# Two layers of a hybrid trunk on one core: the q/k products issued in halves of 256 tokens

## The chip, the cores and the metric
The kernel runs on one core of one Trainium2 chip. Its engines are TensorE (products; the profile calls the product stream PE and the loading of the stationary operand PEld), the vector engine (DVE), the scalar engine (ACT), GpSimd (POOL), and SyncE (SP), which here only issues DMAs. The metric is the device time of one execution in microseconds, as the median of several runs.

## What is computed
The reference runs two layers over 512 tokens of 1024 channels. Per layer:

```python
h = rms_norm(x, pre_norm[layer])
proj = h @ w_in[layer]                       # 8 parts of 1024 columns each
c_b, c_c, c_x, c_z, r_q, r_k, r_v, r_z = split(proj)
y_conv = c_b * causal_depthwise_conv(c_c * c_x, conv_w[layer]) * silu(c_z)
q, k = apply_rotary(r_q), apply_rotary(r_k)  # 8 heads of 128
ret = retention_chunkwise(q, k, r_v)         # chunks of 128 tokens
ret = head_norm(ret) * silu(r_z)
x = x + rms_norm(concat(y_conv, ret) @ w_out[layer], post_norm[layer])
```

Everything is float32. To get that precision from a faster kind of product, each operand is split exactly into a high part and a remainder, and each product of a weight runs in three passes: high by high, high by remainder, remainder by high.

## The kernel before
The weights come in units: a unit of `w_in` holds 256 rows (two blocks of 128 along the contraction) by 512 columns. `units` lists them in the order of use; `fetch` issues their DMAs three units ahead, and `prepare` splits each, the high part `wh` on the scalar engine (L99) and the remainder `wl` on the vector engine (L100).

A layer handles its eight heads in four pairs. For each pair four groups of products run one after the other: v and z of the two heads (the tokens are the stationary operand), q and k of the two heads, and two groups for 128 channels each of the convolution (in these three the weights are the stationary operand and the 512 tokens stream). Each group has four targets, one PSUM bank of 128 x 512 float32 each, and adds up 4 units = 8 blocks of 128 into each; with three passes that is 4 x 8 x 3 = 96 products. After the fourth pair come the products with `w_out`.

`run_units` issues a group: for a step's targets and units, and for the two blocks of a unit, it calls `mm3`, which issues the three passes (L252 to L254). Each pass names its stationary operand anew, so each has a weight load of its own. `stationary_weights` gives the operands of the q/k group: 128 columns of `wh` and `wl` as stationary, `hTh` and `hTl` (high part and remainder of the tokens) as streaming operand. The first pass of a target carries `start`, which makes the bank begin anew, the last one `stop`.

Behind the q/k group `rope` rotates its four targets on the vector engine (L320 to L323). The first convolution group of the pair already runs then, and between its steps stand the scores (L339: small float32 products of 128 columns; the mask on the vector engine is L343) and the transposes of k into its natural layout (L356). Later come the states (L361) and the retention itself (L378, L382), small products too. A scheduler puts the instructions of each engine in order when the program is built, so that work of neighbouring steps can stand in another order than in the code. PSUM has five banks for the groups' targets and three for the small products.

At the start ten products of zeros (L163) run on TensorE while the first loads arrive.

Of the kernel before, what the change touches and what calls it, by code (L numbers as in the profile page):

```python
# [31 lines left out]


def _two_pi_parts():
    """2 * pi in parts (Cody and Waite); n * part is exact for all but the last."""
    rest = 2.0 * np.pi
    parts = []
    for bits in (8, 8, 8):
        e = np.floor(np.log2(abs(rest)))
        q = 2.0 ** (e - bits + 1)  # L40
        part = np.trunc(rest / q) * q
        parts.append(float(part))
        rest -= part
    parts.append(float(np.float32(rest)))
    return parts


# 10000 ** (-i / 64), i < 64, in float32
INV_FREQ = "0000803fd7af5d3f11f93f3fe03d263f9af50f3fcf53f93e9be8d73e1bf8ba3e9be8a13e04358c3e23d4723eed47523e8718363e40b01d3e778d083ed67fec3dcdcccc3d7859b13d0d94993d4dfe843dc255663d3f76473d15ba2c3d4893153de386013dd254e03c4f43c23c8b39a83c39ad913c334d7c3cf27b5a3c11333d3c0ad7233c2de10d3cb0b9f53b15cad43b9c44b83bcc919f3b772e8a3b0e526f3b383e4f3b0f77333b0d691b3b6f94063b2815e93a5cd7c93a8ec9ae3a0e5c973a6f12833ae201633a8c94443a443b2a3a166a133aac4fff392517dd39d774bf3960cba53972928f3915a87839e453573953773a391679213972d40b39e22cf238"

# column offsets in the table of constants
C_INVF = 0
C_MASK = C_INVF + 1
C_ID = C_MASK + P
# [20 lines left out]

@with_exitstack
def hybrid_trunk(ctx: ExitStack, tc, x, x_t, positions, pre_g, post_g, w_in, w_out, conv_w, consts, out):
    """Two layers on one core.

    Every product of a weight runs as three float32r passes over operands split  # L80
    exactly in two (hi + lo). The projection takes h without its factor
    r = rsqrt(mean(x^2) + eps) per token; r is applied behind it. The decays of the
    retention and r are scales of v and of the eps of the head norm.
    """
    nc = tc.nc
    PSUM = bass.MemoryType.PSUM

# [7 lines left out]
    aux = ctx.enter_context(tc.tile_pool(name="aux", bufs=3, space=PSUM))  # L95

    def split(dst_h, dst_l, src):
        """dst_h + dst_l = src, each of 12 significant bits."""
        nc.scalar.activation(out=dst_h, in_=src, func=AF.Copy)  # L99
        nc.vector.tensor_tensor(out=dst_l, in0=src, in1=dst_h.bitcast(F32), op=ALU.subtract)  # L100

# [3 lines left out]
            out=dst_l, in0=src, scalar=scale, in1=dst_h.bitcast(F32), op0=ALU.mult, op1=ALU.subtract  # L105
        )

# [1 line left out]
    units = []  # L109
    for l in range(DEPTH):  # L110
        units += [w_in[l, g, kp] for g in range(NG) for kp in range(NKP)]
# [31 lines left out]
            ws[i] = (wh, wl)  # L143
            fetch(i + 3)

# [1 line left out]
    warm = cpool.tile([P, 1], F32, name="warm")  # L147
    nc.vector.memset(warm, 0.0)
    nc.scalar.activation(out=warm, in_=warm, func=AF.Silu)
# [5 lines left out]
    hTl0 = hpool.tile([P, NK, SEQ], F32R, name="hTl0", tag="hTl")  # L155
    fetch(2)

    # keeps TensorE's clock up until the first operands are there
    zero = tpool.tile([P, D], BF16, name="zero", tag="junk")
    nc.vector.memset(zero[:, :512], 0.0)  # L160
    pz = aux.tile([P, 512], F32, name="pz", tag="aux")
# [28 lines left out]
    def rotary_tables():  # L190
        ang = tpool.tile([P, SEQ], F32, name="ang", tag="sz")
        nn = tpool.tile([P, SEQ], F32, name="nn", tag="acc")
        nc.vector.tensor_copy(out=nn, in_=pos_i)
        nc.vector.tensor_scalar(
            out=ang, in0=nn, scalar1=cst[:, C_INVF : C_INVF + 1], scalar2=None, op0=ALU.mult
        )
        big = 1.5 * 2.0**23
        nc.vector.tensor_scalar(
            out=nn, in0=ang, scalar1=float(1.0 / (2.0 * np.pi)), scalar2=big, op0=ALU.mult, op1=ALU.add
        )  # L200
        nc.vector.tensor_scalar(out=nn, in0=nn, scalar1=big, scalar2=None, op0=ALU.subtract)
        for part in _two_pi_parts():
            nc.vector.scalar_tensor_tensor(
                out=ang, in0=nn, scalar=-part, in1=ang, op0=ALU.mult, op1=ALU.add
            )
        pi = 3.1415925
        nc.vector.tensor_scalar(out=ang, in0=ang, scalar1=pi, scalar2=-pi, op0=ALU.min, op1=ALU.max)
        nc.scalar.activation(out=sin_t, in_=ang, func=AF.Sin)
        # cos(r) = sin(pi/2 - |r|)
        nc.scalar.activation(out=ang, in_=ang, func=AF.Abs)  # L210
        nc.vector.tensor_scalar(
            out=ang, in0=ang, scalar1=-1.0, scalar2=float(np.pi / 2), op0=ALU.mult, op1=ALU.add
        )
        nc.scalar.activation(out=cos_t, in_=ang, func=AF.Sin)

# [1 line left out]
    def square_sum(l, t):  # L217
        junk = tpool.tile([P, D], BF16, name=f"jx_{l}_{t}", tag="junk", bufs=1)
        sq = nc.scalar.activation(out=junk, in_=xt[t], func=AF.Square, accum_out=sx[l][:, t : t + 1])  # L219
# [1 line left out]
            tc.keep_in_program_order(sq)  # L221

    def token_factors(l):
        """r, v's scale and the head norm's eps, for all tokens."""
        vx = rpool.tile([P, NT], F32, name=f"vx{l}", tag="vx", bufs=1)
        rx = rpool.tile([P, NT], F32, name=f"rx{l}", tag="rx", bufs=1)
        r2 = rpool.tile([P, NT], F32, name=f"r2{l}", tag="r2", bufs=1)
        vt = rpool.tile([P, NT, HEADS], F32, name=f"vt{l}", tag="vt", bufs=1)
        et = rpool.tile([P, NT, HEADS], F32, name=f"et{l}", tag="et", bufs=1)
        nc.vector.tensor_scalar(out=vx, in0=sx[l], scalar1=1.0 / D, scalar2=EPS, op0=ALU.mult, op1=ALU.add)  # L230
        nc.gpsimd.tensor_tensor(out=rx, in0=vx, in1=mhalf[:, :NT], op=ALU.pow)
        nc.vector.tensor_tensor(out=r2, in0=rx, in1=rx, op=ALU.mult)
        nc.vector.tensor_tensor(out=vt, in0=vtab, in1=r2.unsqueeze(2).to_broadcast([P, NT, HEADS]), op=ALU.mult)
        nc.vector.tensor_tensor(out=et, in0=etab, in1=vx.unsqueeze(2).to_broadcast([P, NT, HEADS]), op=ALU.mult)
        return rx, vt, et

    def factor_rows(l, rx):
        """r and r^2 of the tokens along the free dimension, on every partition."""
        rb = tpool.tile([P, NT, P], F32, name=f"rb{l}", tag="u", bufs=1, padded_shape=[P, NT, P + 1])
        nc.vector.tensor_copy(out=rb, in_=rx.unsqueeze(2).to_broadcast([P, NT, P]))  # L240
        ps = aux.tile([P, SEQ], F32, name=f"psr{l}", tag="aux")
        for t in range(NT):
            nc.tensor.transpose(out=ps[:, t * P : (t + 1) * P], in_=rb[:, t, :], identity=ident)
        row = cpool.tile([P, SEQ], F32, name=f"row{l}", tag="row")
        row2 = cpool.tile([P, SEQ], F32, name=f"row2{l}", tag="row2")
        nc.scalar.activation(out=row, in_=ps, func=AF.Copy)
        nc.scalar.activation(out=row2, in_=ps, func=AF.Square)
        return row, row2

# [1 line left out]
    def mm3(ps, ah, al, bh, bl, first, last):  # L251
        nc.tensor.matmul(out=ps, lhsT=ah, rhs=bh, start=first, stop=False)  # L252
        nc.tensor.matmul(out=ps, lhsT=ah, rhs=bl, start=False, stop=False)  # L253
# [1 line left out]

    cursor = [0]

    def run_units(steps, targets, operands, hooks=None):
        """ps[t] += sum over the units. A step names units and targets (None: all) and takes
        the units target by target; hooks[i] are traced behind step i."""  # L260
        base = cursor[0]
        n = 1 + max(u for us, _ in steps for u in us)
        ps = {t: mm.tile([P, 512], F32, name=f"mm{base}_{t}", tag="mm") for t in targets}
        for i, (us, ts) in enumerate(steps):
            for t in ts or targets:
                for u in us:
                    wh, wl = ws[base + u]
                    for kk in range(2):
                        mm3(ps[t], *operands(t, 2 * u + kk, wh[:, kk, :], wl[:, kk, :]),
                            u == 0 and kk == 0, u == n - 1 and kk == 1)  # L270
            cursor[0] = base + min([u for later, _ in steps[i + 1 :] for u in later], default=n)
            prepare(cursor[0] + 2)
            for fn in (hooks or {}).get(i, ()):
# [17 lines left out]
            return wh[:, s], wl[:, s], ah[:, k, :], al[:, k, :]  # L291
        return operands

# [1 line left out]
    def take_vz(l, p, ps, rx, vt):  # L295
        vs, zs = [], []
        for t in range(NT):
# [29 lines left out]
    class Retention:  # L327
# [18 lines left out]
            self.sT.append(s)  # L346

        def k_natural(self, a):
            """Columns 32a : 32a + 32 of k, tokens on partitions."""
            if a == 0:  # L350
                self.kn = rpool.tile([P, 2, NT - 1, P], F32, name=f"kn_{self.tag}", tag="kn", bufs=1)
            src = self.kT.rearrange("p h (t j) -> p h t j", j=P)
# [53 lines left out]
                    )  # L406

        def finish(self, a):
            """Columns 32a : 32a + 32 of y, transposed; with the last of them, its parts."""
            if a == 0:  # L410
                self.yT = rpool.tile([P, 2, NT, P], F32, name=f"yT_{self.tag}", tag="yT", bufs=1)
            rows = slice(32 * a, 32 * a + 32)
# [4 lines left out]
                e = slice(4 * self.p, 4 * self.p + 2)  # L417
                split(self.mTh[:, e, :], self.mTl[:, e, :], self.yT.rearrange("p h t d -> p h (t d)"))

# [1 line left out]
    def conv(l, ct, ps, row, row2, mTh, mTl):  # L421
        pc, px, pz, pb = ps
        cc = tpool.tile([P, SEQ], F32, name=f"cc_{l}_{ct}", tag="cc")
# [20 lines left out]
        e = 4 * (ct // 2) + 2 + ct % 2  # L444
        split(mTh[:, e, :], mTl[:, e, :], acc)

# [1 line left out]
    def first_half(l, t, ps, og, post):  # L448
        """Columns 0 : 512 of an output row times the gain, and their part of its mean square + eps."""
        ss = rpool.tile([P, 1], F32, name=f"s0_{l}_{t}", tag="s0", bufs=4)  # L450
        v0 = rpool.tile([P, 1], F32, name=f"v0_{l}_{t}", tag="v0", bufs=4)
        junk = tpool.tile([P, 512], BF16, name=f"j0_{l}_{t}", tag="junk", padded_shape=[P, D])
# [34 lines left out]
            split(hTh[:, ks, s], hTl[:, ks, s], xg)  # L487
        return emit

# [1 line left out]
    hTh, hTl = hTh0, hTl0  # L491
    fac = {}

# [6 lines left out]
    for l in range(DEPTH):  # L500
# [5 lines left out]
        for p in range(NPAIR):  # L506
# [23 lines left out]
            if p == 0:  # L530
# [1 line left out]
                if l == 0:  # L532
                    hooks[0] = [rotary_tables]
                nc.sync.dma_start(out=post, in_=post_g[l : l + 1, :].to_broadcast([P, D]))
            ps = run_units(JOINT, range(4), chans, hooks)
            qT, kT = rope(l, p, ps)
            ret = Retention(l, p, vs, zs, qT, kT, fac["et"], mTh, mTl)

# [43 lines left out]


def _packed(x, positions, pre_norm, w_in, conv_w, w_out, post_norm):
    """The inputs laid out as the kernel reads them."""
    col = lambda kind, i: np.arange(kind * 1024 + i * P, kind * 1024 + (i + 1) * P)
    groups = []
    for p in range(NPAIR):
# [49 lines left out]
```

## Time and profile before

| | |
|---|---|
| median of 3 runs | 943.19 us (942.56, 943.19, 943.34) |
| span of the profiled execution, first to last instruction | 941.0 us; its time outside the span is not listed, 2.2 us lie between it and the median |
| PE | busy 933.1 us (99%), 4338 records |
| PEld | busy 776.0 us (82%), 4338 records |
| DVE, ACT, POOL | busy 596.7, 278.4, 24.6 us (63%, 30%, 3%) |
| granted TensorE clock | 0.998 on average |
| DMA | 96.60 MB, 103 GB/s on average |

The columns of the time line are the start of an instruction from the span's start, its duration, the engine, the line of the code, what it writes and reads, and, in brackets, idle time of the engine ahead of it with what ended it. A product's duration reaches from its start to the modelled end of its results, so products overlap in the record; how many of them pass in a time is told by the distance between two starts. A row with x8 merges eight records in a row of one kind: its start is that of the first, its duration runs to the end of the last. A small float32 product of the code leaves two records.

### The profile page before, as it was taken

Reading aid. Unit: us, or ns where it says so; the run is one execution under the profiler, and the core shown is the slowest. Engines: PE = TensorE matmul, PEld = TensorE weight load, DVE = VectorE, ACT = ScalarE, POOL = GpSimd, SP = SyncE. Lnnn points to the kernel's source line nnn. Section 1 sums busy time; section 2 is a strip of 40 time slices with the busy share of each in tenths; the row PEclk is TensorE's granted clock in tenths of the full one; section 3 lists DMA queues with packets and bytes.
Section 4 is the critical chain, followed back from the end, with each engine's and each line's share of the span. In section 5 each row is a group of like instructions: output and inputs, shape, how many; then the busy total and the mean of one; then the engine's idle time right before and its main releaser. Section 6 shows DMA issues by size and latency. Waiting matters only on the chain.

```text
span 941.0 us, 10986 instructions
## 1 busy us (share of the span) xinstructions
PE 933.1 (99%) x4338; PEld 776.0 (82%) x4338; DVE 596.7 (63%) x960; ACT 278.4 (30%) x450; POOL 24.6 (3%) x46
## 2 busy tenths in 40 slices
PE   9999999999999999999999999999999999999997
PEld 6788888888888888888888888888888888888886
DVE  5595839583958395825764948394849484947324
ACT  5522331222133213324542133213321332222311
POOL 0000000000000000000000000000000000000000
PEclk9999999999999999999999999999999999999999
DMA  8522132213222322235532222322222222222222
GB/s 309 178 92 90 53 127 90 90 63 116 90 90 68 112 90 90 71 108 179 178 122 103 91 90 79 100 90 90 88 92 90 90 90 90 90 91 90 89 68 90
DMA packets 27700, 96.60 MB, mean 103 GB/s; under 512 B 3328, under 2 KB 3456, under 8 KB 27648
## 3 DMA queue, kind: packets, MB, share of 16 engines
q1 hardware_dynamic: 27504, 95.88, 30.7%
q8 instruction: 34, 0.56, 0.2%
q14 instruction: 18, 0.15, 0.1%
q10 hardware_dynamic: 144, 0.01, 0.0%
HBM read 93.78 MB, written 2.10 MB: 102 GB/s over the span
## 4 chain that ended last, share of the span: by engine, by line
PE 94%; DMA 2%; DVE 1%; ACT 1%; issue 1%; POOL 0%; SPq 0%; DVEq 0%; POOLq 0%; ACTq 0%
PE mm L252 30%; PE mm L254 29%; PE mm L253 29%; PE pa L378 2%; PE pss L339 2%; PE pa L382 1%; PE pk L361 1%; DMA xT<-in_x_t 1%; DMA x<-in_x 1%; DVE wl L100 1%; DMA pre_c<-in_pre_norm 0%; DVE x L470 0%; PE psx L481 0%; ACT wh L99 0%; ACT jx L219 0%
## 5 line engine op out<-in xcount | busy, mean ns | idle before, releaser
L100 DVE TENSOR_TENSOR wl<-raw,wh 128x1024 fp32r<-128x1024 f32 (+1 forms) x169 | 205.4, 1217 | 226.5 <-ACT wh L99 222.8
L99 ACT ACTIVATE wh<-raw 128x1024 fp32r<-128x1024 f32 (+1 forms) x169 | 178.1, 1054 | 470.6 <-PE mm L253 303.1
L252 PE MATMUL mm<-hTh,wh 128*128 128x512 f32 x768 | 302.5, 394 | 0.1
L254 PE MATMUL mm<-hTh,wl 128*128 128x512 f32 x768 | 299.8, 390 | 0.3 <-DVE wl L100 0.3
L253 PE MATMUL mm<-hTl,wh 128*128 128x512 f32 x768 | 298.7, 389 | 0.0
L254 PEld LDWEIGHTS mm<-hTh,wl 128*128 128x128 f32 x768 | 144.1, 188 | 31.4 <-DVE wl L100 0.7
L252 PEld LDWEIGHTS mm<-hTh,wh 128*128 128x128 f32 x768 | 144.3, 188 | 29.3 <-ACT z L304 0.6
L253 PEld LDWEIGHTS mm<-hTl,wh 128*128 128x128 f32 x768 | 144.3, 188 | 29.1
L252 PE MATMUL mm<-wh,hTh 128*128 128x512 f32 x256 | 99.6, 392 | 0.3 <-ACT hTh L99 0.3
L253 PE MATMUL mm<-wl,hTh 128*128 128x512 f32 x256 | 99.8, 390 | 0.0
L254 PE MATMUL mm<-wh,hTl 128*128 128x512 f32 x256 | 99.8, 390 | 0.0
L252 PE MATMUL mm<-wh,mTh 128*128 128x512 f32 x256 | 99.8, 390 | 0.0
L254 PE MATMUL mm<-wh,mTl 128*128 128x512 f32 x256 | 99.6, 389 | 0.0
L253 PE MATMUL mm<-wl,mTh 128*128 128x512 f32 x256 | 99.6, 389 | 0.0
L252 PEld LDWEIGHTS mm<-wh,hTh 128*128 128x128 f32 x256 | 48.1, 189 | 11.5 <-ACT wh L99 1.2
L415 DVE STREAM_TRANSPOSE yT<-y 32x256 f32<-32x256 f32 x128 | 55.8, 436 | 2.1
L253 PEld LDWEIGHTS mm<-wl,hTh 128*128 128x128 f32 x256 | 48.1, 188 | 10.5 <-DVE wl L100 0.6
L254 PEld LDWEIGHTS mm<-wh,mTl 128*128 128x128 f32 x256 | 48.0, 188 | 10.1
L254 PEld LDWEIGHTS mm<-wh,hTl 128*128 128x128 f32 x256 | 48.1, 188 | 9.9
L252 PEld LDWEIGHTS mm<-wh,mTh 128*128 128x128 f32 x256 | 48.1, 188 | 9.9
L253 PEld LDWEIGHTS mm<-wl,mTh 128*128 128x128 f32 x256 | 48.1, 188 | 9.9
L356 DVE STREAM_TRANSPOSE kn<-qk 32x192 f32<-32x192 f32 x128 | 47.3, 370 | 2.0
(85 smaller groups left out, 596.3 us busy)
## 6 DMA issues: line engine op xcount, KB each, us to landing
raw<-in_w_in SPq DMA_DIRECT2D x127, 512.0 KB, 3.3
raw<-in_w_out SPq DMA_DIRECT2D x40, 512.0 KB, 3.3
x<-in_x SPq DMA_DIRECT2D x4, 512.0 KB, 7.2
out<-x SPq DMA_DIRECT2D x8, 256.0 KB, 2.1
xT<-in_x_t SPq DMA_DIRECT2D x3, 512.0 KB, 7.7
post<-in_post_norm SPq DMA_DIRECT2D x2, 512.0 KB, 5.5
xT<-in_x_t SPq DMA_DIRECT2D x2, 256.0 KB, 3.9
raw<-in_w_in SPq DMA_DIRECT2D x2, 256.0 KB, 4.2
```

The source lines that it names most:

```text
L99: nc.scalar.activation(out=dst_h, in_=src, func=AF.Copy)
L100: nc.vector.tensor_tensor(out=dst_l, in0=src, in1=dst_h.bitcast(F32), op=ALU.subtract)
L252: nc.tensor.matmul(out=ps, lhsT=ah, rhs=bh, start=first, stop=False)
L253: nc.tensor.matmul(out=ps, lhsT=ah, rhs=bl, start=False, stop=False)
L254: nc.tensor.matmul(out=ps, lhsT=al, rhs=bh, start=False, stop=last)
L339: nc.tensor.matmul(out=pss[:, j, :], lhsT=self.kT[:, h, s], rhs=self.qT[:, h, s], start=True, stop=True)
L356: nc.vector.transpose(out=self.kn[cols, :, :, rows], in_=src[rows, :, : NT - 1, cols])
L361: nc.tensor.matmul(out=pk[:, h, :], lhsT=self.kn[:, h, t, :], rhs=self.vs[t][:, h, :], start=True, stop=True)
L378: nc.tensor.matmul(out=pa[:, j, :], lhsT=self.sT[b][:, j, :], rhs=self.vs[t][:, h, :], start=True, stop=(t == 0))
L382: nc.tensor.matmul(out=pa[:, j, :], lhsT=self.qT[:, h, t * P : (t + 1) * P], rhs=self.S[t][:, h, :], start=False, stop=True,)
L415: nc.vector.transpose(out=self.yT[rows, :, :, cols], in_=self.y[cols, :, :, rows])
```

## The change
`run_units` takes a further argument, `halves`. With the value 2, each block's three passes are issued first for the columns 0 to 255 of the streaming operand and the bank, and then once more for the columns 256 to 511. The q/k groups alone pass 2; all others keep 1. `start` stands on the first pass of the first half alone, `stop` on the last pass of the second half alone.

```diff
-    def run_units(steps, targets, operands, hooks=None):
+    def run_units(steps, targets, operands, hooks=None, halves=1):
...
                 for u in us:
                     wh, wl = ws[base + u]
                     for kk in range(2):
-                        mm3(ps[t], *operands(t, 2 * u + kk, wh[:, kk, :], wl[:, kk, :]),
-                            u == 0 and kk == 0, u == n - 1 and kk == 1)
+                        ah, al, bh, bl = operands(t, 2 * u + kk, wh[:, kk, :], wl[:, kk, :])
+                        for c in range(halves):
+                            s = slice(c * 512 // halves, (c + 1) * 512 // halves)
+                            mm3(ps[t][:, s], ah, al, bh[:, s], bl[:, s],
+                                u == 0 and kk == 0 and c == 0, u == n - 1 and kk == 1 and c == halves - 1)
...
-            ps = run_units(JOINT, range(4), chans, hooks)
+            ps = run_units(JOINT, range(4), chans, hooks, 2)
             qT, kT = rope(l, p, ps)
```

The rest of the diff takes out comments and docstrings. Three lines are added ahead of the later functions, so that L320 becomes L323 and so on; L252 to L254 stay.

On TensorE, where the first q/k group begins (`mm_0_333` is its first target, `wh_232` and `wl_233` the first unit's parts, `wh_262` the second's), there stands before:

```order
L254 MATMUL mm_3_162<-wh_187,hTl_89 128x512
L252 MATMUL mm_0_333<-hTh_88,wh_232 128x512
L253 MATMUL mm_0_333<-hTl_89,wh_232 128x512
L254 MATMUL mm_0_333<-hTh_88,wl_233 128x512
...
L252 MATMUL mm_0_333<-hTh_88,wh_262 128x512
L253 MATMUL mm_0_333<-hTl_89,wh_262 128x512
L254 MATMUL mm_0_333<-hTh_88,wl_263 128x512
```

and now:

```order
L254 MATMUL mm_3_162<-wh_187,hTl_89 128x512
L252 MATMUL mm_0_333<-hTh_88,wh_232 128x256
L253 MATMUL mm_0_333<-hTl_89,wh_232 128x256
L254 MATMUL mm_0_333<-hTh_88,wl_233 128x256
...
L252 MATMUL mm_0_333<-hTh_88,wh_262 128x256
L253 MATMUL mm_0_333<-hTl_89,wh_262 128x256
L254 MATMUL mm_0_333<-hTh_88,wl_263 128x256
```

The three rows of a unit stand twice before (its two blocks) and four times now (two blocks, two halves); over the program TensorE has 4786 rows in place of 4018. The order of targets, units and small products around them is as before.

On the vector engine, behind the rotation of q and k in the second pair of layer 0 (`kn` is k in its natural layout, `wl_1246` the remainder of the last unit of the convolution group that follows), there stands before:

```order
L323 TENSOR_TENSOR qk_1_1_1180<-t_0_1_3_1187,t_0_1_3_1188 128x512
L356 STREAM_TRANSPOSE kn_1_1264<-qk_1_1_1180 32x6x32 x7
L100 TENSOR_TENSOR wl_1246<-raw_1105,wh_1245 128x1024
L356 STREAM_TRANSPOSE kn_1_1264<-qk_1_1_1180 32x6x32
L100 TENSOR_TENSOR wl_1252<-raw_1135,wh_1251 128x1024
L343 TENSOR_TENSOR sT_1_0_1262<-pss_1_0_1257,cst 128x512
```

and now (the names have other numbers):

```order
L326 TENSOR_TENSOR qk_1_1_1372<-t_0_1_3_1379,t_0_1_3_1380 128x512
L359 STREAM_TRANSPOSE kn_1_1456<-qk_1_1_1372 32x6x32 x8
L100 TENSOR_TENSOR wl_1438<-raw_1249,wh_1437 128x1024
L100 TENSOR_TENSOR wl_1444<-raw_1303,wh_1443 128x1024
L346 TENSOR_TENSOR sT_1_0_1454<-pss_1_0_1449,cst 128x512
```

One transpose has gone ahead of the split; pairs 2 and 3 and the second layer show the same. The scalar engine, GpSimd and the DMA queue have the same rows in the same order.

## Rows read from the trace of the kernel before

**Rows 1.** The page: busy times (part 1) and shares of the chain (part 4).

```profile
PE 933.1 (99%) x4338; PEld 776.0 (82%) x4338; DVE 596.7 (63%) x960; ACT 278.4 (30%) x450; POOL 24.6 (3%) x46
...
PE 94%; DMA 2%; DVE 1%; ACT 1%; issue 1%; POOL 0%; SPq 0%; DVEq 0%; POOLq 0%; ACTq 0%
```

**Rows 2.** Waits of PE: who, for whom, us in total, times, longest.

```profile
PE mm L252 <- ACT hTh L99: 0.3, 1, 0.3
PE mm L254 <- DVE wl L100: 0.3, 1, 0.3
```

**Rows 3.** Time line of PE, q/k group of the second pair.

```profile
123.23 0.39 PE L252 MATMUL mm<-hTh,wh 128*128 128x512 f32 x1
...
140.01 0.39 PE L254 MATMUL mm<-hTh,wl 128*128 128x512 f32 x1
...
144.99 0.39 PE L252 MATMUL mm<-hTh,wh 128*128 128x512 f32 x1
```

**Rows 4.** Time line of PEld, same group.

```profile
140.01 0.19 PEld L252 LDWEIGHTS mm<-hTh,wh 128*128 128x128 f32 x1
```

**Rows 5.** Time line of PEld, warm-up products.

```profile
2.05 0.15 PEld L163 LDWEIGHTS <-zero 128*128 128x128 bf16 x1 [0.28 <-issue]
...
4.61 0.15 PEld L163 LDWEIGHTS <-zero 128*128 128x128 bf16 x1 [0.28 <-issue]
```

**Rows 6.** Windows: stretch, its length, busy us, PEclk, DMA share, GB/s.

```profile
0.00:6.00 6.00, 4.78 (x11) 1.84 (x12) 1.39 (x5) 2.73 (x4) 0.20 (x4) 1.00 0.58 184
...
123.00:145.00 22.00, 22.00 (x99) 18.21 (x98) 8.31 (x10) 4.65 (x7) 0.00 (x0) 1.00 0.30 98
```

**Rows 7.** Time line of PE, a burst of small products.

```profile
86.03 1.05 PE L361 MATMUL pk<-v,kn 128*128 128x128 f32 x8
86.92 0.83 PE L378 MATMUL pa<-v,sT 128*128 128x128 f32 x6
87.59 0.39 PE L382 MATMUL pa<-S,qk 128*128 128x128 f32 x2
87.81 0.39 PE L378 MATMUL pa<-v,sT 128*128 128x128 f32 x2
```

**Rows 8.** Groups of PEld by line: busy us, mean ns of one, idle before.

```profile
L253 PEld LDWEIGHTS mm<-hTl,wh 128*128 128x128 f32 x768 | 144.3, 188 | 29.1
```

**Rows 9.** Time line of PE around a burst of scores.

```profile
62.14 0.40 PE L254 MATMUL mm<-hTh,wl 128*128 128x512 f32 x1
62.38 1.05 PE L339 MATMUL pss<-qk,qk 128*128 128x128 f32 x8
...
63.50 0.39 PE L253 MATMUL mm<-hTl,wh 128*128 128x512 f32 x1
...
65.81 0.39 PE L254 MATMUL mm<-hTh,wl 128*128 128x512 f32 x1
66.03 0.39 PE L252 MATMUL mm<-hTh,wh 128*128 128x512 f32 x1
...
67.85 0.39 PE L254 MATMUL mm<-hTh,wl 128*128 128x512 f32 x1
```

**Rows 10.** Time line of PEld, q/k group of the first pair.

```profile
28.02 0.19 PEld L252 LDWEIGHTS mm<-hTh,wh 128*128 128x128 f32 x1
...
31.85 0.19 PEld L254 LDWEIGHTS mm<-hTh,wl 128*128 128x128 f32 x1 [0.70 <-DVE wl L100]
```

**Rows 11.** Time line of DVE and PE behind the second pair's q/k group.

```profile
153.65 0.69 DVE L323 TENSOR_TENSOR qk<-t,t 128x512 f32<-128x512 f32 x1
...
157.07 1.23 DVE L100 TENSOR_TENSOR wl<-raw,wh 128x1024 fp32r<-128x1024 f32 x1
158.32 0.37 DVE L356 STREAM_TRANSPOSE kn<-qk 32x192 f32<-32x192 f32 x1
...
155.88 1.05 PE L339 MATMUL pss<-qk,qk 128*128 128x128 f32 x8
...
163.39 0.39 PE L253 MATMUL mm<-hTl,wh 128*128 128x512 f32 x1
```

## The prediction, on record before the changed kernel was run
> **What bounds the kernel now.** I read the page first: TensorE's product stream is busy for 99% of the span, and in the chain of waits it holds 94%, with the DMA at 2% and the vector engine at 1% [rows 1]. The waits view says the same from the other side: behind the warm-up the product stream waited for another engine twice in the whole run, 0.3 us each time [rows 2]. So nothing that another engine does can be won or lost here unless it grows into a new wait; the time is the number of products times the distance from one product's start to the next (the pitch). The third view is therefore the time line of TensorE inside a q/k group. In the second pair of layer 0 the 96 products of the group start at 123.23 and the first product after them at 144.99: 21.76 / 96 = 226.7 ns each, with no hole [rows 3]. A product's own duration there (0.39 us) is not its price, because the products overlap; only starts count.
>
> The loads tell what stands between two products. Each product has a load of its own, and the load of the next one starts within 10 ns of the start of the present one (both at 140.01), so loads lie under products [rows 3, 4].
>
> **What 227 ns consist of.** The ten warm-up products, also of 512 columns, start every (4.61 - 2.05) / 6 = 427 ns [rows 5]. That is 1.2 columns per ns, one column per clock of the lower of the two levels; I go by this pitch although the windows view prints 1.00 for that stretch too. In the q/k group the granted clock is 1.00 (2.4 GHz) [rows 6], where one column per clock is 213.3 ns for 512 columns. So 226.7 is 213.3 of streaming and 13.3 of something else (my estimate from these rows). All of the forecast hangs on what that 13.3 belongs to: to the product as an instruction with its load, or to its 512 columns.
>
> **What the change adds and moves.** The groups concerned are 2 layers x 4 pairs = 8; each has 4 targets x 8 blocks of the contraction x 3 passes = 96 products of 512 columns. They become 192 of 256 columns: 768 products and 768 loads more in the run, columns unchanged. The loads are repeated, since each half has its three passes to itself. No other engine gets or loses an instruction.
> - Product term, bounded below: the shortest pitch that a load and its product show here is that of the small fp32 products of 128 columns, eight from 86.03 to 86.92, 111 ns, and two from 87.59 to 87.81, 110 ns [rows 7]. A half can hardly go below that, as its load is as large as theirs: 2 x 111 - 226.7 = -4.7 ns per old product, x 768 = -3.6 us.
> - Bounded above: if a product had to wait for the recorded end of its load (188 ns [rows 8]), two halves would cost 376, +149 ns x 768 = +115 us. Rows 7 rule this out: the small products load as many weights and run at 111. The nearer upper row is the one that shows a 512 column product at its slowest without a wait: the last one ahead of a burst of small products starts at 62.14 and the burst at 62.38 [rows 9]. With the rounding that is 0.23 to 0.25 us; I take 235 ns, 21.7 over the streaming. Two halves with that on each are 256.7, +30 x 768 = +23.0 us.
> - What I take: the 13.3 goes to each half, 106.7 + 13.3 = 120.0, so 240.0 for 226.7, +13.3 x 768 = +10.2 us. My reason is in the rows after a burst: the same 512 column products run at (65.81 - 63.50) / 10 = 231 ns for ten starts and fall back to (67.85 - 66.03) / 8 = 227.5 ns, and the one ahead of a burst, whose next load is of another kind, takes 235 [rows 9]. No wait stands there and columns and clock are the same; what differs is which load lies under the product. A cost that moves with the load is a cost per load, and the change doubles the loads.
>
> Here the Trainium skill speaks against me: its page "TensorE: Matmul & The Clock Gate" (Part 2, step 1) says that loading the next weights doesn't take read bandwidth from the running product. Rows 9 don't agree for this kernel, since a product's pitch moves by 4 to 8 ns or more with the load beside it; by the rule the 13.3 would not double with the loads, which leads to the second and third rivals.
>
> - Waits: the first pair of layer 0 already waits for its weights inside the q/k group (0.70 us before the load at 31.85, with the group's first load at 28.02) [rows 10]. Between these, (31.85 - 0.70 - 28.02) / 0.227 = some 13 products run, so slower halves hide 13 x 13.3 ns = 0.2 us of it. Sum: +10.2 - 0.2 = +10.0 us.
> - The moved vector instructions: in pairs 1 to 3 of each layer one 0.37 us transpose goes ahead of the remainder split that ran from 157.07 to 158.30 [rows 11]; behind that split stand the next one and the masking of the scores. In the product order that remainder is first used behind the second burst of scores, after 163.39 [rows 11]. Some 5 us of cover, so 0.4 us costs nothing (pair 0 has like moves of at most 0.7 us); without cover it would be 0.37 x 6 = 2.2 us.
> - The rotation of q and k must end (153.65 + 0.69 = 154.34) before the scores at 155.88 [rows 11]: 1.5 us of cover. It follows the completion of the first target, which in the changed order lies 18 x 2 halves ahead of the group's end, 18 x 13.3 ns = 0.24 us earlier against that end than now. The cover grows; nothing is won from it, since TensorE doesn't wait there.
>
> The profiled execution has a span of 941.0 us, 2.2 us under the median of the runs (943.19), and I carry that difference over: 941.0 + 10.0 + 2.2 = 953.2 us.
>
> **Rivals.**
> 1. The halves pay more than the whole does. The 226.7 is a settled rhythm; a 512 column product outside it costs 231 to 235 [rows 9], 17.7 to 21.7 over streaming. With 107 ns of streaming over a load that needs 110 there may be no slack to settle in. Each half then 124.4 to 128.4, +22 to +30 ns per old product, +17 to +23 us: 960 to 966. Against it: the small products, which have as little slack, are perfectly even [rows 7].
> 2. The 13.3 belongs to the columns (213.3 x 17/16 = 226.7), so a half costs 113.3, just over its load's 111, and nothing changes: 943.2, give or take 1.5. For it: small products carry only 111 - 106.7 = 4 ns over what 256 clocks would be, so a large fixed cost per load is not visible there. Against it: rows 9.
> 3. A small fixed cost per instruction (4.3 ns as in rows 7) beside a part that goes with the columns: (13.3 - 4.3) / 2 + 4.3 = 8.8 over 106.7, so 231.0 for two, +4.3 x 768 = +3.3 us: 946.5. The same page of the Trainium skill ("Back-to-back issue gap") gives the column time plus 2.5 ns as the gap; by its figure the change would cost an estimated 2.5 x 768 = 1.9 us. The trace's 226.7 is not that gap either, so no run here shows the rule at this shape.
> 4. Faster: the whole 13.3 is tied to the long stream, and halves run at the pace of loads alone, 111 ns as the small products do [rows 7]: -3.6 us, 939.6. It decides if products of 256 columns start within 113 ns of each other; place: all eight q/k groups. For it, rows 7 are the only rows with that much streaming per load; against it, those are another kind of product, whose four-byte operands are taken in another way (two records for each product of the code).
> That the change doesn't do what it says is out: the changed order has the 768 further products, and the halves stand next to each other.
>
> **How the numbers follow.** Forecast (a half at 118 to 124 ns, 951 to 957 with 953.2 in the middle) 0.52; rival 1 0.14; rival 2 0.17; rival 3 and what lies between it and the forecast 0.08; rival 4 0.09. A measurement of this kernel can tell about 0.2% (1.9 us) from no change. Faster is rival 4: 0.09. Same is rival 2 with the lowest part of rival 3: 0.18. Slower is the rest: 0.73. For the range I leave out rival 4 (below 941.5) and the upper half of rival 1 (above 963): 941.5 to 963.
>
> **What would show it.** In the changed profile the starts inside a q/k group: 120 ns apart is the forecast, 113 rival 2, 111 rival 4, 124 and more, or uneven starts, rival 1. The products' idle time should stay under 2 us and the starts outside the q/k groups at 227 ns; the q/k group of the second pair should last 23.0 us in place of 21.8. A q/k group that grows by a wait for a load's operand, or a gap ahead of the scores, would make the working wrong even if the time came out.

## The result and the profile after

The changed kernel takes 953.23 us (median of 4 runs, 952.29 to 953.62), the kernel before 943.27 us beside it (942.56 to 943.39). The ratio is 1.0105 with a 95% interval of 1.009 to 1.012: slower by 10.0 us. The profiled execution has a span of 951.6 us, 10.6 over the 941.0 of before.

The page of the changed kernel shows 768 products and 768 loads more than [rows 1], and nothing else of size. Part 1 and the engine line of part 4:

```profile
PE 943.2 (99%) x5106; PEld 816.2 (86%) x5106; DVE 596.1 (63%) x960; ACT 278.3 (29%) x450; POOL 24.5 (3%) x46
...
PE 94%; DMA 2%; DVE 1%; issue 1%; ACT 1%; SPq 0%; POOL 0%; DVEq 0%; POOLq 0%; ACTq 0%
```

The time line of PE in the second pair's q/k group, which answers to [rows 3], from its first product to the seventh of the group behind it:

```profile
124.75 0.28 PE L252 MATMUL mm<-hTh,wh 128*128 128x256 f32 x1
124.86 0.28 PE L253 MATMUL mm<-hTl,wh 128*128 128x256 f32 x1
124.98 0.28 PE L254 MATMUL mm<-hTh,wl 128*128 128x256 f32 x1
125.10 0.28 PE L252 MATMUL mm<-hTh,wh 128*128 128x256 f32 x1
...
140.10 0.28 PE L254 MATMUL mm<-hTh,wl 128*128 128x256 f32 x1
...
147.78 0.40 PE L252 MATMUL mm<-hTh,wh 128*128 128x512 f32 x1
...
149.17 0.39 PE L252 MATMUL mm<-hTh,wh 128*128 128x512 f32 x1
```

The 192 halves take 147.78 - 124.75 = 23.03 us, 120.0 ns each, where the 96 whole products took 21.76, at a granted clock of 1.00 (2.4 GHz) in both. From the fourth start on they stand 0.12 us apart without exception; the first two distances are shorter by up to 7 ns. The loads keep the same distance and still start with the product ahead (PEld, answering to [rows 4]):

```profile
140.10 0.19 PEld L252 LDWEIGHTS mm<-hTh,wh 128*128 128x128 f32 x1
140.22 0.19 PEld L253 LDWEIGHTS mm<-hTl,wh 128*128 128x128 f32 x1
```

The 10.6 us of span, worked out group by group from the starts in the two time lines: the six q/k groups of the later pairs +1.27 us each, that of layer 1's first pair +1.23, that of layer 0's first pair +1.52, together +10.4. Each convolution group behind a q/k group is 0.03 us longer (+0.2 in all), because the first 512 column products behind the halves start 233 ns apart or so before they settle (149.17 - 147.78 = 1.39 for six, 1.36 when settled). The start of the kernel was 0.1 us shorter. All other groups are as long as before to 0.04 us, but for 0.08 us in the first one, which waits for its data.

The first pair's +1.52 holds a wait that grew, here on the time line of PEld:

```profile
32.38 0.19 PEld L254 LDWEIGHTS mm<-hTh,wl 128*128 128x128 f32 x1 [1.10 <-DVE wl L100]
```

In [rows 10] the same wait was 0.70 us and ended at 31.85. What came later is a block of `x`: the scalar engine squares it ahead of the split of the weights, and its time line shows the square at 26.13 before and at 26.67 in the changed kernel, in both behind a DMA, and the split behind it (L99) 0.53 us later:

```profile
26.13 1.06 ACT L219 ACTIVATE jx<-x 128x1024 bf16<-128x1024 f32 x1 [0.20 <-DMA x<-in_x]
...
28.46 1.05 ACT L99 ACTIVATE wh<-raw 128x1024 fp32r<-128x1024 f32 x1
```

```profile
26.67 1.06 ACT L219 ACTIVATE jx<-x 128x1024 bf16<-128x1024 f32 x1 [1.15 <-DMA x<-in_x]
...
28.99 1.04 ACT L99 ACTIVATE wh<-raw 128x1024 fp32r<-128x1024 f32 x1
```

Another wait of the same group shrank. Before, a load further on waited 0.58 us for `z` on the scalar engine (the row below); in the changed kernel the load that answers to it, at 33.72, begins 0.09 us behind the end of the one ahead of it. Taken from the starts of the products, as what they stand apart beyond their settled pitch, the first wait cost some 0.56 us before and 1.15 now, the second 0.45 before and 0.14 now:

```profile
33.20 0.19 PEld L252 LDWEIGHTS mm<-hTh,wh 128*128 128x128 f32 x1 [0.58 <-ACT z L304]
```

### The profile page after: what moved, and what is told of

Same layout as the page of the kernel before. It is cut to its first block, busy times and chain, and to the rows that moved or that the text cites. A ratio compares the mean times of both kernels' runs of the same rounds, so it can differ in the third digit from the quotient of the medians.

```text
span 951.6 us, 12546 instructions
## 1 busy us (share of the span) xinstructions
PE 943.2 (99%) x5106; PEld 816.2 (86%) x5106; DVE 596.1 (63%) x960; ACT 278.3 (29%) x450; POOL 24.5 (3%) x46
## 4 chain that ended last, share of the span: by engine, by line
PE 94%; DMA 2%; DVE 1%; issue 1%; ACT 1%; SPq 0%; POOL 0%; DVEq 0%; POOLq 0%; ACTq 0%
PE mm L252 30%; PE mm L254 30%; PE mm L253 29%; PE pa L381 2%; PE pss L342 1%; PE pa L385 1%; PE pk L364 1%; DMA xT<-in_x_t 1%; DMA x<-in_x 1%; DVE wl L100 0%; DVE x L473 0%; PE psx L484 0%; ACT wh L99 0%; ACT jx L219 0%; POOL r L469 0%
## 5 line engine op out<-in xcount | busy, mean ns | idle before, releaser
L252 PE MATMUL mm<-hTh,wh 128*128 128x512 f32 (+1 forms) x1024 | 347.8, 340 | 0.0
L254 PE MATMUL mm<-hTh,wl 128*128 128x512 f32 (+1 forms) x1024 | 345.0, 337 | 0.9 <-DVE wl L100 0.9
L253 PE MATMUL mm<-hTl,wh 128*128 128x512 f32 (+1 forms) x1024 | 344.1, 336 | 0.0
L99 ACT ACTIVATE wh<-raw 128x1024 fp32r<-128x1024 f32 (+1 forms) x169 | 178.0, 1054 | 481.0 <-PE mm L253 309.6
L254 PEld LDWEIGHTS mm<-hTh,wl 128*128 128x128 f32 x1024 | 194.3, 190 | 21.9 <-DVE wl L100 1.1
L253 PEld LDWEIGHTS mm<-hTl,wh 128*128 128x128 f32 x1024 | 194.6, 190 | 19.3
L252 PEld LDWEIGHTS mm<-hTh,wh 128*128 128x128 f32 x1024 | 194.5, 190 | 19.0
L252 PE MATMUL mm<-wh,mTh 128*128 128x512 f32 x256 | 99.8, 390 | 0.0
L254 PE MATMUL mm<-wh,hTl 128*128 128x512 f32 x256 | 99.8, 390 | 0.0
L254 PE MATMUL mm<-wh,mTl 128*128 128x512 f32 x256 | 99.6, 389 | 0.0
L252 PE MATMUL mm<-wh,hTh 128*128 128x512 f32 x256 | 99.3, 391 | 0.3 <-ACT hTh L99 0.3
L252 PEld LDWEIGHTS mm<-wh,hTh 128*128 128x128 f32 x256 | 47.9, 188 | 11.2 <-ACT wh L99 1.0
L418 DVE STREAM_TRANSPOSE yT<-y 32x256 f32<-32x256 f32 x128 | 55.8, 436 | 2.1
L254 PEld LDWEIGHTS mm<-wh,mTl 128*128 128x128 f32 x256 | 48.0, 188 | 10.0
L254 PEld LDWEIGHTS mm<-wh,hTl 128*128 128x128 f32 x256 | 48.1, 188 | 9.9
L252 PEld LDWEIGHTS mm<-wh,mTh 128*128 128x128 f32 x256 | 48.1, 188 | 9.9
```

Of the source, the lines that this page charges most:

```text
L254: nc.tensor.matmul(out=ps, lhsT=al, rhs=bh, start=False, stop=last)
L418: nc.vector.transpose(out=self.yT[rows, :, :, cols], in_=self.y[cols, :, :, rows])
```

## The experiments

By then the size was known: 13.3 ns for each further product. Open was what the 13.3 belongs to (the q/k groups, a change of the stationary operand, the load, the product itself) and where it ends. In the first three experiments the time counts, in the last two the pitch of series of products that are put behind the work.

**All groups in halves.** One character against the changed kernel:

```diff
-    def run_units(steps, targets, operands, hooks=None, halves=1):
+    def run_units(steps, targets, operands, hooks=None, halves=2):
```

> All 40 groups of products run in halves, not only the 8 q/k groups: 3840 products of 512 columns become 7680 of 256. Fixed-cost theory (each product costs its columns plus 13.3 ns, whatever its length): +13.3 ns x 3840 = +51.2 us over the kernel before, 994.5 us, less up to 1 us that the waits of the start hide; starts 120 ns apart in every group, also where the tokens are the stationary operand. Rival, a cost of the q/k groups alone (their operands, or what the vector engine does beside them): the other groups' halves would run nearer to 113 ns, and the time would stay within a few us of the changed kernel's 953.2.

Measured: 992.43 us against 942.72 (ratio 1.0526, 1.0508 to 1.0543), +49.7. In a group whose stationary operand is the tokens the 192 halves take (129.45 - 106.41) / 192 = 120.0 ns:

```profile
106.41 0.28 PE L252 MATMUL mm<-wh,hTh 128*128 128x256 f32 x1
...
129.45 0.28 PE L252 MATMUL mm<-hTh,wh 128*128 128x256 f32 x1
```

Five times the products cost five times the time, so the cost isn't one of the q/k groups. The 1.5 us that are missing from +51.2 lie mostly behind the 32 bursts of small products of the pairs: there 24 whole products take 232.3 ns each on average until the next burst, and 48 halves 121.5 to 121.7, so that a product costs 11 ns more in place of 13.3 (24 x 2.3 x 32 = 1.8 us).

**The halves pass by pass.** The two halves of a pass stand next to each other, with the same stationary operand:

```diff
-                        for c in range(halves):
-                            s = slice(c * 512 // halves, (c + 1) * 512 // halves)
-                            mm3(ps[t][:, s], ah, al, bh[:, s], bl[:, s],
-                                u == 0 and kk == 0 and c == 0, u == n - 1 and kk == 1 and c == halves - 1)
+                        passes = ((ah, bh), (ah, bl), (al, bh))
+                        for w, (lw, rh) in enumerate(passes):
+                            for c in range(halves):
+                                s = slice(c * 512 // halves, (c + 1) * 512 // halves)
+                                nc.tensor.matmul(
+                                    out=ps[t][:, s], lhsT=lw, rhs=rh[:, s],
+                                    start=u == 0 and kk == 0 and w == 0 and c == 0,
+                                    stop=u == n - 1 and kk == 1 and w == 2 and c == halves - 1,
+                                )
```

> The q/k groups run in halves as in the changed kernel, but pass by pass: the two halves of a pass stand next to each other, so the same stationary operand is named twice in a row. Fixed-cost theory, with a load for every product: nothing changes against the changed kernel, 953.2 us, 768 loads more than before and starts 120 ns apart. Rival, that what costs is the exchange of one stationary operand for another: every second product has nothing to exchange and runs at 107 to 111 ns, so a pair costs 227 to 231 and the time goes back to 943 to 947 us.

Measured: 952.43 us against 942.72 (1.0102, 1.0087 to 1.0117), the changed kernel's ratio. The q/k group of the second pair lasts 147.02 - 123.99 = 23.03 us, as in the changed kernel. Its page has 5106 loads, as many as the changed kernel's:

```profile
PE 943.1 (99%) x5106; PEld 816.8 (86%) x5106; DVE 596.6 (63%) x960; ACT 278.5 (29%) x450; POOL 24.6 (3%) x46
```

The program loads the operand again for each float32r product, even where it is the one already there, and the product pays the same. The rival of the exchange is out.

**Uneven halves, 320 and 192 columns.**

```diff
+                        cuts = (0, 320, 512) if halves == 2 else (0, 512)
                         for c in range(halves):
-                            s = slice(c * 512 // halves, (c + 1) * 512 // halves)
+                            s = slice(cuts[c], cuts[c + 1])
```

> The q/k groups' products are cut into 320 and 192 columns in place of 256 and 256; columns, products and loads are as many as in the changed kernel. Fixed cost alone: 146.7 + 93.3 = 240.0 ns for a pair, 953.2 us as the changed kernel. Fixed cost, but no product faster than a load (111 ns): 146.7 + 111 = 257.7, +31.0 ns x 768 = +23.8 us over the kernel before, 967.0 us. Rival, all of the cost goes with the columns: 226.7, or with the floor 141.7 + 111 = 252.7 and 963.2 us; the starts inside a q/k group tell the two with a floor apart (147 against 142 ns behind the long part's start).

Measured: 967.64 us against 942.72 (1.0267, 1.0252 to 1.0282), +24.9 where the fixed cost with a floor gives +23.8. The time line of PE in the second pair's q/k group: its first product, a stretch of one block (three passes of each part), and the first product of the group behind it:

```profile
126.41 0.30 PE L252 MATMUL mm<-hTh,wh 128*128 128x320 f32 x1
...
127.16 0.33 PE L252 MATMUL mm<-hTh,wh 128*128 128x320 f32 x1
127.33 0.31 PE L253 MATMUL mm<-hTl,wh 128*128 128x320 f32 x1
127.47 0.31 PE L254 MATMUL mm<-hTh,wl 128*128 128x320 f32 x1
127.62 0.25 PE L252 MATMUL mm<-hTh,wh 128*128 128x192 f32 x1
...
151.14 0.41 PE L252 MATMUL mm<-hTh,wh 128*128 128x512 f32 x1
```

The group takes 151.14 - 126.41 = 24.73 us, and that over its 96 pairs is 257.6 ns a pair: 257.7 was expected of the fixed cost with a floor, 252.7 of a cost that goes with the columns. The start of the first long part behind the short ones is put early in the record (127.16 and then 0.17), so single starts tell less: the long part's later ones, 127.33, 127.47 and 127.62, stand some 145 to 147 ns apart, which leans to 147 against 142. The columns, products and loads are those of the changed kernel, and the time grows by 24.9 us where that grows by 10.0: a floor is there. Changing lengths is not what costs, for the series below, each of one length, add up to the same (146.3 + 111.3 = 257.6 for 320 and 192 columns).

**Series of products by themselves.** The kernel before with a function that runs 24 equal products in a row behind the last group; the core of it:

```diff
+        def series(name, n, cols, lhs, rhs, same=False, nb=8, count=24):
+            pp = aux.tile([P, 512], F32, name=name, tag="aux")
+            for i in range(count):
+                w = lhs[:, 0 if same else i % nb, 0:cols]
+                m = nc.tensor.matmul(out=pp[:cols, 0:n], lhsT=w, rhs=rhs[:, (i + 3) % nb, 0:n], start=True, stop=True)
+                tc.keep_in_program_order(m)
```

> The kernel before, with 31 series of 24 products of their own behind the last group (their results are read by nobody): the pitch in each series is read from the trace, the time of the whole says nothing. With float32r operands and a stationary operand of 128 columns, the fixed-cost theory gives columns / 2.4 + 13.3 ns down to the floor of a load: 512: 226.7, 448: 200.0, 384: 173.3, 320: 146.7, 288: 133.3, 256: 120.0, and 111 for 224, 192 and 128. A cost that goes with the columns gives 198.3, 170.0, 141.7, 127.5, 113.3. Stationary operands of 96, 64 and 32 columns under products of 256 and 512: if the 13.3 is what the load costs column by column, 10.0, 6.7 and 3.3 ns remain over 106.7 and 213.3 (116.7, 113.3, 110.0 and 223.3, 220.0, 216.7); if it is a cost of the product itself or of any load, 120.0 and 226.7 stay. bfloat16 operands (512, 256, 128 columns): smaller loads, so by the load theory 3 to 7 ns over the columns in place of 13.3; by a cost per product 13.3 again.

The time line of PE, one row for each series (x24); the pitch is the distance to the start of the next series over 24. `r` is a float32r product with a full load (the number is its columns), `rw` and `rv` are products of 256 and 512 columns over loads of the number's columns, `b` is bfloat16; `rsamex` has the same stationary operand 24 times; `ronetilex` and `bsamex` stand only as the ends of the series ahead of them:

```profile
934.43 5.60 PE L498 MATMUL r512x<-mTh,mTl 128*128 128x512 f32 x24
939.87 5.03 PE L498 MATMUL r448x<-mTh,mTl 128*128 128x448 f32 x24
944.73 4.35 PE L498 MATMUL r384x<-mTh,mTl 128*128 128x384 f32 x24
948.92 3.67 PE L498 MATMUL r320x<-mTh,mTl 128*128 128x320 f32 x24
952.43 3.33 PE L498 MATMUL r288x<-mTh,mTl 128*128 128x288 f32 x24
955.60 3.04 PE L498 MATMUL r256x<-mTh,mTl 128*128 128x256 f32 x24
958.47 2.84 PE L498 MATMUL r224x<-mTh,mTl 128*128 128x224 f32 x24
961.14 2.83 PE L498 MATMUL r192x<-mTh,mTl 128*128 128x192 f32 x24
963.81 2.81 PE L498 MATMUL r128x<-mTh,mTl 128*128 128x128 f32 x24
966.46 2.97 PE L498 MATMUL rw96x<-mTh,mTl 128*96 128x256 f32 x24
969.27 5.69 PE L498 MATMUL rv96x<-mTh,mTl 128*96 128x512 f32 x24
974.80 2.90 PE L498 MATMUL rw64x<-mTh,mTl 128*64 128x256 f32 x24
977.54 5.67 PE L498 MATMUL rv64x<-mTh,mTl 128*64 128x512 f32 x24
983.05 2.89 PE L498 MATMUL rw32x<-mTh,mTl 128*32 128x256 f32 x24
985.78 5.72 PE L498 MATMUL rv32x<-mTh,mTl 128*32 128x512 f32 x24
991.33 3.03 PE L498 MATMUL rsamex<-mTh,mTl 128*128 128x256 f32 x24
994.20 5.63 PE L498 MATMUL ronetilex<-mTh 128*128 128x512 f32 x24
999.67 5.35 PE L498 MATMUL b512x<-hb 128*128 128x512 bf16 x24
1004.86 2.78 PE L498 MATMUL b256x<-hb 128*128 128x256 bf16 x24
1007.48 1.50 PE L498 MATMUL b128x<-hb 128*128 128x128 bf16 x24
1008.82 2.78 PE L498 MATMUL bsamex<-hb 128*128 128x256 bf16 x24
```

With full loads: 512 columns (939.87 - 934.43) / 24 = 226.7 ns, 448 202.5, 384 174.6, 320 146.3, 288 132.1, 256 119.6, and 111.3, 111.3 and 110.4 for 224, 192 and 128. Less columns / 2.4 that is 13.3, 15.8, 14.6, 13.0, 12.1, 12.9, and then the floor. So the cost is fixed within 2 or 3 ns over these lengths, and with full loads it doesn't go with the columns: 256 columns would stand at 113.3. The products of the series carry `start` and `stop` each and add nothing up in the bank, and their pitch is that of the kernel's products, so adding up is not what costs. With the same operand 24 times it is 119.6 ns, as with operands in turn.

Smaller loads do what the load theory says in part. Under 256 columns a load of 96, 64 or 32 columns leaves 117.1, 114.2 and 113.8 ns: the first two steps are those expected (116.7, 113.3), the third (110.0) is not. Under 512 columns the same loads leave 230.4, 229.6 and 231.3, more than the full load, where the theory expected less. (A smaller load here also means fewer rows of the bank written; the series don't part the two.) In bfloat16 the pitch is 216.3, 109.2 and 55.8, 2.5 to 3 ns over the columns at all three lengths, with a load for each product too.

All this is one execution. Seven of the lengths with full loads (448 to 192 columns) ran a second time in it, further on, and came out within 0.5 ns of the first.

**Mixed kinds, and loads of 2 columns.** The same function, and pairs of a float32r and a bfloat16 product in turn:

```diff
+            for i in range(count):
+                k = nc.tensor.matmul(out=pp[:, 0:n], lhsT=ml[:, i % 8, 0:P], rhs=mh[:, (i + 3) % 8, 0:n], start=True, stop=True)
+                tc.keep_in_program_order(k)
+                k = nc.tensor.matmul(out=pq[:, 0:m], lhsT=hb[:, i % 4, 0:P], rhs=hb[:, (i + 3) % 4, 0:m], start=True, stop=True)
+                tc.keep_in_program_order(k)
```

> The kernel before with other series of 24 products behind the last group (results read by nobody, the time of the whole says nothing). Two series alternate a float32r product with a bfloat16 product of the same length, so that under each lies the load of the other kind. If the load is what lengthens the product above it: the float32r product (bfloat16 load under it) runs at 215.8 of 512 columns, or 109 of 256, the bfloat16 product (float32r load under it) at 226.7 or 120. If the extra is the float32r product's own: the other way round, 226.7 and 120 for float32r, 215.8 and 109 for bfloat16. If both have to be float32r: both near 215.8 and 109. Then stationary operands of 64, 32 and 2 columns under float32r products of 512 to 192 columns: by the load theory with 2 columns nearly nothing is left over columns / 2.4 (216, 162, 136, 109, 82); if the extra goes with the streamed columns once the load is short, 230 for 512 and 113 for 256 stay as with 32 columns (17 and 7 ns over). Last, 480, 416, 352 and 272 columns with full loads: 213.3, 186.7, 160.0, 126.7 if the 13.3 is a constant, up to 3 ns more or less if it is one only at some lengths, as 448 (203.0) and 288 (131.7) of the first probe let expect.

The time line of PE: first two mixed pairs of 512 columns, then a series of 256 columns over loads of 32 (`c32n256x`; the row behind it is its end), series over loads of 2 columns (`c2n`), and the series behind them:

```profile
940.08 0.39 PE L507 MATMUL x512b<-hb 128*128 128x512 bf16 x1
940.12 0.58 PE L505 MATMUL x<-mTh,mTl 128*128 128x512 f32 x1
940.54 0.39 PE L507 MATMUL x512b<-hb 128*128 128x512 bf16 x1
...
983.31 2.99 PE L498 MATMUL c32n256x<-mTh,mTl 128*32 128x256 f32 x24
986.14 2.28 PE L498 MATMUL c32n192x<-mTh,mTl 128*32 128x192 f32 x24
988.26 5.66 PE L498 MATMUL c2n512x<-mTh,mTl 128*2 128x512 f32 x24
993.75 4.36 PE L498 MATMUL c2n384x<-mTh,mTl 128*2 128x384 f32 x24
997.95 3.65 PE L498 MATMUL c2n320x<-mTh,mTl 128*2 128x320 f32 x24
1001.44 2.96 PE L498 MATMUL c2n256x<-mTh,mTl 128*2 128x256 f32 x24
1004.24 2.32 PE L498 MATMUL c2n192x<-mTh,mTl 128*2 128x192 f32 x24
1006.40 5.38 PE L498 MATMUL r480x<-mTh,mTl 128*128 128x480 f32 x24
1011.62 4.69 PE L498 MATMUL r416x<-mTh,mTl 128*128 128x416 f32 x24
1016.15 4.00 PE L498 MATMUL r352x<-mTh,mTl 128*128 128x352 f32 x24
```

The mixed pairs didn't tell the two apart. The record puts the start of the float32r product early (0.04 us behind the bfloat16 product's), so only a pair can be read: 0.46 us, 230 ns a product, more than 226.7 + 216.3 = 443 ns for the two by themselves. At 256 columns a pair takes 243 ns where the two by themselves take 119.6 + 109.2 = 228.8. All three expectations are missed; putting the kinds in turn costs something of its own.

The loads of 2 columns do tell: 228.8, 175.0, 145.4, 116.7 and 90.0 ns for 512, 384, 320, 256 and 192 columns, that is 15.4, 15.0, 12.1, 10.0 and 10.0 over the columns. With almost nothing to load, 10 to 15 ns stay; against full loads that is 2.1 ns more at 512 columns and 2.9 ns less at 256. Loads of 64 and 32 columns, in the same run, lie between 10.0 and 13.3 over the columns at 384 and 320. How far such small differences can be read is told by 256 columns over loads of 32: (986.14 - 983.31) / 24 = 117.9 ns here, 113.8 in the first series run. So 4 ns between two series with small loads decide nothing.

At 192 columns the small loads take the floor away: with full loads 111.3 ns, with loads of 32 columns (988.26 - 986.14) / 24 = 88.3 and of 2 columns 90.0. The floor goes with the load; the fewer rows of the bank that a small load leaves to write don't explain it, for bfloat16 products of 128 columns write all 128 rows and take 55.8.

The last three rows fit the fixed cost: 217.5 ns for 480 columns and 188.8 for 416 (4.2 and 2.1 more than columns plus 13.3), and 159.6 for 352 (to the next series, at 1019.98), 12.9 over the columns.

## Why the prediction was right, and where its reasons failed

1. *What bounds the kernel.* Right. But for the first pair's waits the time moved with the number of products alone; the products of all groups apart from q/k kept their pitch, the first six behind each q/k group excepted (0.03 us).
2. *The product term, 768 x 13.3 = +10.2 us.* Right: 120.0 ns a half, and +1.27 us for an undisturbed group where 96 x 13.3 ns = 1.28. The split of 226.7 into 213.3 and 13.3 was the step that carried it, with the choice that each half pays the 13.3. The series confirm both at seven further lengths (480 to 288 columns) within some 4 ns.
3. *The reason given for it, a cost that goes with the load.* Not borne out. It rested on [rows 9], where products are slower after a burst and ahead of one. The series over loads of 2 columns keep 10 to 15 ns, so most of the cost stays where there is next to nothing to load. What [rows 9] show is that the extra wanders for some starts behind a burst; the products behind a series of halves, which are of the same kind and have the same loads, do so too (233 ns or so). That each float32r product pays the 13.3 is shown, and the forecast needs no more; whether it is paid for the load or for the product itself stays open, because a float32r product comes with a load in every run here. Having a load of any kind isn't enough, for the bfloat16 products have one each and keep 2.5 to 3 ns. The prediction set its reason against the rule in "TensorE: Matmul & The Clock Gate" of the Trainium skill (Part 2, step 1) that a load takes no bandwidth from the running product; the series give no steady ground for that objection, since a smaller load shortens the pitch by 2 to 6 ns under 256 columns and lengthens it by 2 to 5 under 512.
4. *The waits.* Wrong in sign: -0.2 us was forecast for the first pair, and its group grew by 0.25 us more than an undisturbed one (+1.52 against +1.27). A part of the waiting did go away: the wait for `z`, which the prediction didn't count, cost some 0.3 us less. But the first wait, which was to lose 0.2 us, cost 0.6 us more and ended 0.53 us later, because the block of `x` on which the split hangs came later in this execution. Such times move where no code has changed: in the two series runs, whose kernel up to the last group is that of before, the wait is 0.77 and 1.00 us in place of 0.70, and the square of that block starts at 25.68 and 26.52 in place of 26.13. (Whether the change itself has a part in the delay isn't shown.) So the term was mis-sized because it took one execution's landing time for fixed. The 0.45 us between forecast and result lie within the spread of the changed kernel's runs (1.3 us).
5. *The moved vector instructions and the cover of the scores.* Right: behind the first pair's q/k group no group grew by a wait.
6. *Rivals.* Rival 1 (unsettled halves) is out: the halves stand 120 ns apart from the fourth start of an undisturbed group on. Rival 2 (113.3) is out by the changed kernel and by the series with full loads. Rival 3 names the 2.5 ns of the Trainium skill's page "TensorE: Matmul & The Clock Gate" ("Back-to-back issue gap"), given there for products by themselves, without their loads: the figure holds here for bfloat16 products with a load each (2.5 to 3 ns) and not for float32r (13.3). Rival 4 put the floor at the right place, 111 ns, but of the lengths that ran a product reaches it at 224 columns and below; at 256 the fixed cost keeps it 8 to 9 ns above. The prediction read the 111 ns of the small products as 4 ns over 256 clocks of streaming; float32r products of 224, 192 and 128 columns take the same 111, so it is the pitch of a full load and says nothing of the fixed cost of longer products.
7. *The sum.* The forecast of 953.2 us hits the measured 953.23 closer than its working can. The span grew by 10.6 us, 0.6 more than the sum of +10.0; the 2.2 us carried over from the span to the median came out as 1.6 (953.23 - 951.6). That the two cancel is luck.

## What to carry to other kernels

Where TensorE's product stream has no holes, the time is products times pitch, so read the pitch from starts, split it into columns and a rest, and ask of any cut of the products how often the rest is paid. For float32r here the rest is 13.3 ns: longest products are best, halving costs 6%, and from 224 columns down a product with a full load of 128 columns takes 111 ns whatever its length. In these programs a load is repeated for each such product even over the same operand, so putting halves with one operand side by side saves nothing.

## What the runs showed of the hardware that was not expected

- Float32r products over full loads settle at a pitch of columns / 2.4 + 13.3 ns at 512, 384, 352, 320 and 256 columns (226.7, 173.3, 160.0, 146.7 and 120.0 ns once settled); at 480, 448, 416 and 288 the distances go on changing, and their average is 12 to 17 ns over the columns. Bfloat16 products stand 2.5 to 3 ns over the columns.
- The floor of 111 ns goes with a full float32r load: 192 columns take 111.3 ns over it and 88 to 90 over loads of 32 or 2 columns.
- With 512 columns a smaller load makes a float32r product slower: 226.7 ns over 128 loaded columns, 230 over 96 or 64, 229 to 231 over 32 or 2. At 384 and 320 columns it does not (173 to 175 and 143 to 146 ns, with full loads 174.6 and 146.3).
- A float32r and a bfloat16 product in turn take 460 ns a pair at 512 columns, 17 ns more than the two by themselves.
- After a burst of small products whole products need about ten starts to come back to 226.7 ns, halves three to eight to come back to 120; whole products behind halves need six.
